# One Hymba layer on one core: key halves in all rows, tied 1/rms copies, and down's first operands in up's used tiles

## The chip, the cores and the metric

One core of a Trainium2 chip runs the kernel. Five engines take part, each with its own queue of instructions that it works off in order: TensorE (PE; its weight loads are shown apart as PEld), VectorE (DVE), ScalarE (ACT), GpSimd (POOL) and SyncE (SP), which only issues transfers. ACT and POOL issue transfers too. The metric is the device time of one execution in microseconds (us); lower is better. The instructions' times come from one profiled execution.

## What is computed

One inference step of one decoder layer, for 1024 prompt tokens and 8 x 8 decode tokens (1088 in all), width 1024, in f32. Cut to what matters:

```python
hn = rms_norm(x, norm_mix_gain)
proj = hn @ w_in                       # q,k,v,gate of retention; q,k,v of attention
o_r = rms_norm(retention(q_r, k_r, v_r, state)) * silu(g_r)
q_s = rms_norm(q_s, q_norm_gain); k_s = rms_norm(k_s, k_norm_gain)
o_s = windowed attention, 128 wide, 8 query heads on 2 key heads of 64, ALiBi, a sink logit per head
h = x + concat(o_r, o_s) @ w_out
hf = rms_norm(h, norm_ffn_gain)
h = h + square(relu(hf @ w_up)) @ w_down      # w_up 1024 x 4096, w_down 4096 x 1024
```

## The kernel before, in words

**Two halves for each f32.** PE multiplies a reduced format of f32 here (F32R). So an f32 operand is kept as a high part, rounded to that format, and a low part, the rest. `halve` (L754, L755) makes them: an ACT cast for the high one, a DVE subtraction for the low one. `mm3` (L178 to L180) is a product of two such pairs: high times high, low times high, high times low, three matmuls into one bank. Low times low is left out.

**Front.** The input is loaded and normalised. `spread` (L171 to L173) writes the tokens' 1/rms to memory (r_d) and reads them back along the free axis of all partitions (rsb). Then `proj_q` projects the first queries, and a loop over nine token tiles of 128 (L307 on) projects attention's keys and values: 24 matmuls of 256 columns into `pst`, the key's norm (hsq on ACT, hr and kn on DVE, a reciprocal root on POOL), a transposition on PE into `ptk` (L325), and the copies. `kh2[kv]` holds the high half of key head kv, 64 rows long, twice: ACT copies it (L331) to rows 0 to 63 and to rows 64 to 127. `kl` holds the low halves, one key head in each 64 rows, made by DVE (L332). All of them lie in one tile (kk).

**Attention.** `swa_block(c)` treats 128 queries, first for key head 0, then for 1, a half block each. The queries `qx` hold the high part in one half of the rows and the low part in the other (L392, L393). For each of four heads L400 multiplies all 128 rows of qx with kh2 (high and low query by high key in one matmul) and L401 the 64 high rows with the 64 rows of kl. DVE adds the bias (L402) and takes the maximum, ACT the exponentials, POOL multiplies by the reciprocal sums (L366), PE transposes the probabilities (L371) and multiplies them with the values (L420). Between these steps PE takes matmuls of other projections (psf, psg) as filler. The decode tokens come after block 7. They need `r8s`, 1/rms of the 64 decode tokens in another order, copied from rsb in 8 copies (L431); `col_sums` (L436 on) reads them.

**Up and down.** After retention and the output projection, `up(fp)` does 16 tiles of the wide MLP in a Strassen-like scheme: 7 products (PROD) on combinations of weights and activations, for two halves s of the tokens. Operands 1, 2, 6, 5, 7, 4, 3 lie in pools ops0 and ops1 as high and low tiles of 4 x 272. `left` loads a weight tile in two raw halves (`rawload`, on ACT's queue), makes the combinations on POOL (`comb`, L962) and splits them (`wsplit`). The results are squared on ACT (L1028), combined for down by four POOL subtractions for each s (L1063) and stored to u_d (L1068). Down works in five groups of 2, 4, 4, 4 and 2 such tiles; per group it does the products 1, 6, 7, 4, 5, 3, 2 (DOWN). For each it loads the activations `ur` from u_d on SP's queue (L1098), halves them into `uh` and `ul`, takes the next weight combination of each tile and issues mm3 for 4 x 2 outputs into `psd` banks; ACT copies or DVE adds them to the accumulators (L1116, L1118). In the group of two tiles a product is 4 x 2 x 2 x 3 = 48 matmuls.

**Order.** The program is written stage by stage; a scheduler with a model of the engines' times then decides, at build, the order of each engine's queue. Reading the source therefore doesn't give the order around up's end, nor of L431; the built kernel does. Tiles with the same tag share buffers: the next use waits for the last reader of the one before.

## Time and profile before

| what | before |
|---|---|
| median of 3 runs | 1283.24 us (1282.28 to 1283.95) |
| profiled execution, its span | 1280.67 us, 1278.9 us |
| mean granted PE clock | 0.981 |
| DMA | 169.45 MB, mean 133 GB/s |
| attention (100 to 300 us): PE busy | 200.00 of 200 us |

Views that are used: the page (busy time of each engine over the span); windows (busy time of each engine in a stretch, PE's granted clock as a share of full, the share of the 16 DMA engines); the timeline (start, duration, engine, line, operation, output<-inputs, and in brackets the idle time before it and what ended it); groups by line (busy time and mean ns, then idle time before them); one line's instructions (durations min/median/max in ns, rows x columns in use); waits by engine and line; and the chain, the work that led up to a point in time, step by step. A matmul's duration holds its way through the array; how fast matmuls follow one another is the difference of two starts.

### The profile page before, as it was taken

The page shows a single profiled execution, that of the slowest core. Times are in us where ns is not written, and L with a number is a line of the kernel's source. Part 1 is how long each engine was busy: PE and PEld are TensorE (multiplying, and loading weights), DVE is VectorE, ACT ScalarE, POOL GpSimd, SP SyncE. Part 2 cuts the span into 40 slices and gives each one's busy share as a digit, 9 for nine tenths or more (in the row PEclk, how much of TensorE's full clock was granted, in tenths as well). Part 3 has the DMA queues.
Part 4 walks back from the last instruction along what each step waited for, and adds up shares of the span by engine and source line. Part 5 has one row for each costly group of instructions (what it writes and reads, how often), then busy time and mean ns, then how long its engine had stood idle before and what let it go on. Part 6 is the DMA issues. An engine that isn't in the chain of part 4 may idle for free.

```text
span 1278.9 us, 23839 instructions
## 1 busy us (share of the span) xinstructions
PE 1221.7 (96%) x9621; PEld 1156.2 (90%) x9621; DVE 838.3 (66%) x1492; ACT 499.8 (39%) x1031; POOL 545.7 (43%) x463
## 2 busy tenths in 40 slices
PE   7979999999999899879999999999589999999998
PEld 5979877788979799879999999999589999999998
DVE  8735655553115787887666666766367778887766
ACT  6333343364304334444444344434264332332331
POOL 8425223123323554667565656665571321413000
PEclk9989999999989999899999999999889999999999
DMA  6211221424402944332443434333575455553124
GB/s 229 68 56 53 85 74 61 156 73 135 121 18 89 301 152 148 113 113 85 154 152 131 146 143 155 139 133 140 188 262 178 137 171 157 180 181 122 55 69 175
DMA packets 97669, 169.45 MB, mean 133 GB/s; under 512 B 11487, under 2 KB 67743, under 8 KB 97303
## 3 DMA queue, kind: packets, MB, share of 16 engines
q1 hardware_dynamic: 85783, 125.46, 29.0%
q10 hardware_dynamic: 9216, 33.56, 8.1%
q0 software_dynamic: 2560, 8.91, 2.2%
q8 instruction: 75, 1.23, 0.4%
q14 instruction: 35, 0.29, 0.1%
HBM read 114.30 MB, written 53.61 MB: 131 GB/s over the span
## 4 chain that ended last, share of the span: by engine, by line
PE 75%; DVE 9%; DMA 7%; POOL 3%; issue 3%; ACT 2%; SPq 0%; ACTq 0%; DVEq 0%; POOLq 0%
PE psd L179 8%; PE psd L180 8%; PE psd L178 8%; PE psx L178 4%; PE psx L180 4%; PE psx L179 4%; PE psf L180 3%; PE psf L178 3%; PE psf L179 3%; POOL rt L1063 2%; DMA u_d<-rt 2%; PE pst L178 2%; PE psz L178 2%; PE psz L180 2%; PE psz L179 2%
## 5 line engine op out<-in xcount | busy, mean ns | idle before, releaser
L178 PE MATMUL psd<-uh,wd_w 128*128 128x272 f32 x896 | 259.5, 290 | 17.7 <-ACT uh L754 17.7
L179 PE MATMUL psd<-uh,wd_w 128*128 128x272 f32 x896 | 260.0, 291 | 0.1
L180 PE MATMUL psd<-ul,wd_w 128*128 128x272 f32 x896 | 256.7, 289 | 0.8 <-DVE ul L755 0.8
L178 PEld LDWEIGHTS psd<-uh,wd_w 128*128 128x128 f32 x896 | 170.8, 191 | 18.1 <-ACT uh L754 18.1
L179 PEld LDWEIGHTS psd<-uh,wd_w 128*128 128x128 f32 x896 | 169.7, 189 | 0.3 <-DVE wd_w L755 0.3
L180 PEld LDWEIGHTS psd<-ul,wd_w 128*128 128x128 f32 x896 | 168.7, 189 | 1.1 <-DVE ul L755 1.1
L1118 DVE TENSOR_TENSOR a<-a,psd 128x272 f32<-128x272 f32 x248 | 102.2, 432 | 46.8 <-PE psd L180 46.7
L755 DVE TENSOR_TENSOR wu_w<-wu_s,wu_w 128x512 fp32r<-128x512 f32 x64 | 62.1, 973 | 84.6 <-ACT wu_w L754 84.4
L755 DVE TENSOR_TENSOR ul<-ur,uh 128x1088 fp32r<-128x1088 f32 x56 | 87.5, 1591 | 15.2 <-ACT uh L754 15.2
L754 ACT CAST wd_w<-wd_s 128x512 fp32r<-128x512 f32 x64 | 37.6, 621 | 112.9 <-PE psd L180 101.7
L178 PE MATMUL psx<-op_0h,wu_w 128*128 128x272 f32 x256 | 75.1, 293 | 0.7 <-ACT m L1040 0.7
L366 POOL TENSOR_TENSOR sp<-sp,ssp 128x1024 f32<-128x1024 f32 (+1 forms) x16 | 28.6, 1789 | 109.9 <-DVE ssp L365 109.9
L180 PE MATMUL psx<-op_0l,wu_w 128*128 128x272 f32 x256 | 74.3, 290 | 0.0
L178 PE MATMUL psx<-op_1h,wu_w 128*128 128x272 f32 x256 | 74.3, 290 | 0.0
L180 PE MATMUL psx<-op_1l,wu_w 128*128 128x272 f32 x256 | 74.1, 289 | 0.0
L179 PE MATMUL psx<-op_0h,wu_w 128*128 128x272 f32 x256 | 74.0, 289 | 0.0
L179 PE MATMUL psx<-op_1h,wu_w 128*128 128x272 f32 x256 | 73.7, 288 | 0.0
L754 ACT CAST uh<-ur 128x1088 fp32r<-128x1088 f32 x56 | 59.5, 1101 | 22.9 <-DMA ur<-u_d 12.4
L962 POOL TENSOR_TENSOR wd_s<-wd_r,wd_s 128x512 f32<-128x512 f32 x16 | 24.0, 1501 | 104.0 <-DVE wd_w L755 101.7
L1027 DVE SCALAR_TENSOR_TENSOR m<-m,rsf 128x272 f32<-128x272 f32 x96 | 65.5, 683 | 3.1
L180 PE MATMUL psf<-hnl,wqk_hi 128*128 128x384 f32 (+1 forms) x192 | 64.9, 338 | 0.0
L178 PE MATMUL psf<-hnh,wqk_hi 128*128 128x384 f32 (+1 forms) x192 | 64.8, 338 | 0.0
(318 smaller groups left out, 3818.8 us busy)
## 6 DMA issues: line engine op xcount, KB each, us to landing
u_d<-rt SPq DMA_DIRECT2D x32, 952.0 KB, 6.1
ur<-u_d SPq DMA_DIRECT2D x56, 544.0 KB, 5.0
wu_r<-in_w_up ACTq DMA_DIRECT2D x32, 512.0 KB, 4.3
wd_r<-in_w_down ACTq DMA_DIRECT2D x32, 512.0 KB, 5.9
y<-in_xY POOLq DMA_DIRECT2D x16, 272.0 KB, 3.3
y_d<-y POOLq DMA_DIRECT2D x16, 272.0 KB, 3.7
yt<-y_d SPq DMA_DIRECT2D x16, 272.0 KB, 3.3
out_yT<-a SPq DMA_DIRECT2D x16, 272.0 KB, 2.2
```

The costliest lines, as they stand in the source:

```text
L178: nc.tensor.matmul(ps, lh, rh, start=first, stop=False, skip_group_check=more)
L179: nc.tensor.matmul(ps, ll, rh, start=False, stop=False, skip_group_check=more)
L180: nc.tensor.matmul(ps, lh, rl, start=False, stop=last, skip_group_check=more)
L366: nc.gpsimd.tensor_tensor(s, s, ss.unsqueeze(2).broadcast_to([P, 4, n]), ALU.mult)
L754: nc.scalar.copy(hi, src)
L755: lo_eng.tensor_tensor(lo, src, hi.bitcast(F32), ALU.subtract)
L962: nc.gpsimd.tensor_tensor(t_, p_, q_, op)
L1027: nc.vector.scalar_tensor_tensor(t_, src, 0.0, rsf[:, s, h, :], ALU.max, ALU.mult)
L1063: sub = lambda o_, p_, q_: nc.gpsimd.tensor_tensor(o_, p_, q_, ALU.subtract)
L1118: nc.vector.tensor_tensor(to, to, ps, ALU.add)
```

## The change

Three edits. First, the 8 copies of L431 are tied behind the DVE instruction that ends `swa_block(5)`. Second, the low half of the keys is kept for each key head in all 128 rows (a second tile, `kl`, beside the old place), so DVE makes four subtractions for each of 8 token tiles instead of two, and the second score matmul takes all rows of qx; with this it also adds low query times low key, which was left out before. Third, the pool `ope` takes the tiles of the s = 0 operands 1, 2, 6 and 5 and outlives up. In the last `up(15)`, `first_down(1, ...)` behind product 2 and `first_down(6, ...)` behind product 5 read the activations of down's products 1 and 6 (from u_d[0], the first two tiles) and the two raw halves of the second weight tile w_down[1] into four of those tiles each, on ACT's queue, and halve the activations there. In down's groups the raw weights of all tiles but a group's first then cycle through these 8 tiles instead of 9 buffers of their own.

```diff
@@ -297,7 +297,7 @@
         square_sum(rsb[:, 768:1088], xs[2][:, k, :], k, "m2")
     sl8 = slot(8, F32R, "kk")
     kh2 = [sl8[:, kv * 1024 : kv * 1024 + 1024] for kv in range(2)]
-    kl = sl8[:, 2048:3072]
+    kl2 = [sl8[:, 2048:3072], sp.tile([P, 1024], F32R, tag="kl", name="kl", bufs=1)]
     for c, (c0, cw) in enumerate(CH):
         acc = rsb[:, c0 : c0 + cw]
         inv_rms(acc, OFFS[c], rst[:, 3 * c : 3 * c + 3], f"m{c}")
@@ -329,9 +329,9 @@
                 p_ = slice(kv * 64, kv * 64 + 64)
                 for d_ in (p_, slice(64 - kv * 64, 128 - kv * 64)):
                     nc.scalar.activation(kh2[kv][d_, cols], pt[p_], AF.Copy, scale=qkg[p_, 1:2])
-                nc.vector.scalar_tensor_tensor(
-                    kl[p_, cols], pt[p_], qkg[p_, 1:2], kh2[kv][p_, cols].bitcast(F32), ALU.mult, ALU.subtract
-                )
+                    nc.vector.scalar_tensor_tensor(
+                        kl2[kv][d_, cols], pt[p_], qkg[p_, 1:2], kh2[kv][p_, cols].bitcast(F32), ALU.mult, ALU.subtract
+                    )
             nc.vector.tensor_scalar(vs[:, t, :], ps[:, 128:256], rt, None, ALU.mult)
         if t == 7:
             nc.vector.tensor_scalar(k8[:, 0:128], pt, qkg[:, 1:2], None, ALU.mult)
@@ -398,7 +398,7 @@
                 for g in (2 * gg, 2 * gg + 1):
                     pg = ps[:, (g % 2) * 256 : (g % 2) * 256 + n]
                     nc.tensor.matmul(pg, qx[:, g, :], kh2[kv][:, k0 : k0 + n], start=True, stop=False)
-                    nc.tensor.matmul(pg, qx[p_, g, :], kl[p_, k0 : k0 + n], start=False, stop=True)
+                    nc.tensor.matmul(pg, qx[:, g, :], kl2[kv][:, k0 : k0 + n], start=False, stop=True)
                     nc.vector.scalar_tensor_tensor(
                         s[:, g, :], dtab[:, 256 - n :], nsl[:, c, kv, g : g + 1], pg, ALU.mult, ALU.add
                     )
@@ -421,17 +421,17 @@
                     po[p_, :], vs[:, c - 1 + h, p_], pts[kv][:, h, :], start=h == halves[0], stop=h == 1
                 )
         nc.scalar.copy(mh, po)
-        nc.vector.tensor_tensor(ml, po, mh.bitcast(F32), ALU.subtract)
+        ins = nc.vector.tensor_tensor(ml, po, mh.bitcast(F32), ALU.subtract)
         mix_store(mh, ml, c * 128, 128)
-
-    for c in range(NB):
-        swa_block(c)
-
-    for c_ in range(8):
-        nc.vector.tensor_copy(
-            r8s[0:1, :, :].rearrange("p t (b c i) -> p t b c i", b=2, c=8)[:, :, :, c_, :],
-            rsb[0:1, 1024:1088].rearrange("p (t b i) -> p t b i", t=4, b=2),
-        )
+        return ins
+
+    done_swa = [swa_block(c) for c in range(NB)]
+    with tc.issue_after(done_swa[5].ins):
+        for c_ in range(8):
+            nc.vector.tensor_copy(
+                r8s[0:1, :, :].rearrange("p t (b c i) -> p t b c i", b=2, c=8)[:, :, :, c_, :],
+                rsb[0:1, 1024:1088].rearrange("p (t b i) -> p t b i", t=4, b=2),
+            )
 
 
     pr = psB.tile([P, 512], F32, tag="t2", name="prq8")
@@ -760,7 +760,12 @@
         return w
 
     def rawload(src, name, tag="raw", pl=None):
-        raw = (pl or mw).tile([P, 1024], F32, tag=tag, name=name, bufs=9 if tag == "rawb" else 3)
+        if tag == "rawb":
+            t_ = ope.tile([P, 4, Q], F32, tag="op" + ("1h", "6h", "2h", "2l", "5h", "5l", "6l", "1l")[kept[0] % 8], name=name)
+            raw = t_.rearrange("p k n -> p (k n)")[:, :1024]
+            kept[0] += 1
+        else:
+            raw = mw.tile([P, 1024], F32, tag=tag, name=name, bufs=3)
         nc.scalar.dma_start(raw, src)
         return raw
 
@@ -942,18 +947,22 @@
 
     opx = ExitStack()
     ops = [[None, None] for _ in range(7)]
+    ope = ctx.enter_context(pool("ope", side="left"))
+    kept = [0]
 
     def operand_tiles(s):
         opp = opx.enter_context(pool(f"ops{s}", side="left"))
-        for i in PROD:
+        for n, i in enumerate(PROD):
             ops[RIGHT[i]][s] = [
-                opp.tile([P, 4, Q], F32R, tag=f"op{i}{x}", name=f"op{RIGHT[i]}_{s}{x}") for x in "hl"
+                (ope if s == 0 and n < 4 else opp).tile([P, 4, Q], F32R, tag=f"op{i}{x}", name=f"op{RIGHT[i]}_{s}{x}")
+                for x in "hl"
             ]
 
-    def left(order, src, name, lo_eng, raw_tag="raw", raw_pool=None, s_tag="S", s_pool=None, tags=("wa", "wb")):
-
-        r1 = rawload(src[:, :1024], f"{name}_r1", raw_tag, raw_pool)
-        r2 = rawload(src[:, 1024:], f"{name}_r2", raw_tag, raw_pool)
+    def left(order, src, name, lo_eng, raw_tag="raw", raw_pool=None, s_tag="S", s_pool=None, tags=("wa", "wb"), raws=None):
+
+        r1, r2 = raws or (
+            rawload(src[:, i * 1024 : i * 1024 + 1024], f"{name}_r{i + 1}", raw_tag, raw_pool) for i in range(2)
+        )
         a11, a12, a21, a22 = r1[:, :512], r1[:, 512:], r2[:, :512], r2[:, 512:]
         have = {1: a11, 2: a12, 4: a22}
 
@@ -1055,6 +1064,10 @@
                 if i == 4:
                     act(tq("v", s), bk, s, 0, rt[s][:, B21, :])
                     held["v", s] = None
+                if fp == 15 and s == 1 and i == 2:
+                    first_down(1, ("1h", "1l", "2h", "2l"))
+                if fp == 15 and s == 1 and i == 5:
+                    first_down(6, ("6h", "6l", "5h", "5l"))
                 if i == 3:
                     t_ = add(6, s, bk)
                     r12 = um.tile([P, Q], F32, tag="r12", name=f"r12{fp}_{s}", bufs=2)
@@ -1067,6 +1080,24 @@
                     sub(r[:, T4, :], r[:, B21, :], r[:, T2, :])
                     nc.sync.dma_start(u_d[fp // 2][:, fp % 2, s, :, :], r)
 
+    begun, raws1 = {}, []
+
+    def first_down(j, tags):
+
+
+        u_raw, raw, u_hi, u_lo = (
+            ope.tile([P, 4, Q], dt, tag="op" + tag, name=f"{n}0_{j}")
+            for n, tag, dt in zip(("ur", "rw", "uh", "ul"), tags, (F32, F32, F32R, F32R))
+        )
+        u_hi, u_lo, u_raw = (v.rearrange("p (f s) n -> p f s n", f=2) for v in (u_hi, u_lo, u_raw))
+        nc.scalar.dma_start(u_raw, u_d[0][:, :, :, RIGHT[j], :])
+        raw = raw.rearrange("p k n -> p (k n)")[:, :1024]
+        h = len(raws1) * 1024
+        nc.scalar.dma_start(raw, a["w_down"][1][:, h : h + 1024])
+        raws1.append(raw)
+        halve(u_hi, u_lo, u_raw, nc.vector)
+        begun[j] = u_hi, u_lo
+
     for fp in range(16):
         up(fp)
     opx.close()
@@ -1083,18 +1114,23 @@
         ur = dn.tile([P, 4, 2, Q], F32, tag="ur", name=f"ur{g}_{i}", bufs=2)
         return ur, [dn.tile([P, 4, 2, Q], F32R, tag=f"u{x}", name=f"u{x}{g}_{i}", bufs=2) for x in "hl"]
 
-    first_tiles = act_tiles(0, 1)
+    first_tiles = act_tiles(0, 7)
     accs[0] = dn.tile([P, 4, 2, Q], F32, tag="a0", name="a0")
     for g, (f0, nf) in enumerate(((0, 2), (2, 4), (6, 4), (10, 4), (14, 2))):
         gens = []
         for f in range(nf):
             own = ("rawb", dn, "Sb", dn) if f else ("raw", mw, "S", mid)
-            gens.append(left(DOWN, a["w_down"][f0 + f], f"wd{f0 + f}", nc.vector, *own, tags=("wb" if f % 2 else "wa",)))
+            gens.append(left(
+                DOWN, a["w_down"][f0 + f], f"wd{f0 + f}", nc.vector, *own, tags=("wb" if f % 2 else "wa",),
+                raws=raws1 if (g, f) == (0, 1) else None))
         banks = {}
         for i in DOWN:
             ws = [next(gen) for gen in gens]
-            ur, uu = first_tiles if g == 0 and i == 1 else act_tiles(g, i)
-            for f in range(0, nf, 2):
+            if g == 0 and i in begun:
+                uu = begun[i]
+            else:
+                ur, uu = first_tiles if g == 0 and i == 7 else act_tiles(g, i)
+            for f in () if g == 0 and i in begun else range(0, nf, 2):
                 nc.sync.dma_start(ur[:, f : f + 2], u_d[(f0 + f) // 2][:, :, :, RIGHT[i], :])
                 halve(uu[0][:, f : f + 2], uu[1][:, f : f + 2], ur[:, f : f + 2], nc.vector)
             q_ = INTO[i]
```

Where instructions go. DVE in the key stage, before (kn, the key times its 1/rms, is what PE transposes; hr and hsq belong to the norm of a key; q2v holds r8s and the values):

```order
L318 TENSOR_SCALAR hr<-hr,rst 128x2 [waits Pool_49]
L320 TENSOR_TENSOR kn<-pst,hr 128x128 [waits DVE_49,PE_49]
L335 TENSOR_SCALAR q2v<-pst,rst 128x128
L332 SCALAR_TENSOR_TENSOR kk<-ptk,c_qkg,kk 64x128 [waits PE_49,Activation_49]
L431 COPY q2v<-rsb 1x8x8 [waits DMAHW5_49]
L431 COPY q2v<-rsb 1x8x8 x3
L315 TENSOR_REDUCE hr<-hsq 128x2 [waits Activation_49]
L431 COPY q2v<-rsb 1x8x8 x4
```

and DVE in the changed kernel, where the copies stand now, at the end of attention's sixth block (row 359 of the queue, where before they began at row 82; ml is the low part of a block's output):

```order
L393 TENSOR_TENSOR qxp_1_2059<-q2v,qxp_1_2059 64x512 [waits Activation_49]
L351 TENSOR_REDUCE mxp_1_1974<-sp_1_1959 128x4 [waits DVE_49]
L424 TENSOR_TENSOR ml_1806<-po_1899,mh_1805 128x512 [waits DMAHW1_49,Activation_49]
L431 COPY q2v<-rsb 1x8x8 x8
L353 TENSOR_TENSOR mxp_1_1974<-mxp_1_1974,rq 128x4 [waits DVE_49]
L413 COPY ptp_0_1943<-ppp_0_1950 128x512 [waits PE_49]
```

The copies left the place between a tile's L332 and the next tile's L315, with the wait for the transfer.

ACT at up's end, before (m715_1 is a copy of up's product 7, which frees a bank for PE; rt15_0, rt15_1 and r1215_0, r1215_1 are squared results of the last tile, the latter two those that POOL's subtractions wait for; wd2_r2 and wd3_r2 are raw halves of down's third and fourth weight tiles):

```order
L1040 COPY m715_1_10098<-psx1_9927 128x272 [waits PE_49]
L754 CAST wd0_w7_10353<-wd0_s7_10351 128x512
L1028 ACTIVATE rt15_0_9932<-m715_0_10081 128x272 [waits DVE_49]
L1028 ACTIVATE rt15_1_9933<-m715_1_10098 128x272 [waits DVE_49]
L1028 ACTIVATE rt15_0_9932<-v15_0_10118 128x272 [waits DVE_49]
L1028 ACTIVATE r1215_0_10154<-m615_0_10021 128x272 [waits DVE_49,Activation_49]
L754 CAST wd0_w4_10424<-wd0_r2_10195 128x512 [waits DMAHW6_49,PE_49]
L1028 ACTIVATE rt15_1_9933<-v15_1_10133 128x272 [waits DVE_49]
L764 DMA wd2_r2_10719<-in_w_down 128x1024 [waits DVE_49]
L1028 ACTIVATE r1215_1_10175<-m615_1_10035 128x272 [waits DVE_49]
```

and in the changed kernel (uh0_6 is the high half of the activations of group 0, product 6, cast from ur0_6):

```order
L754 CAST uh0_6_10094<-ur0_6_10092 128x1088 [waits DMAHW5_49]
L1049 COPY m715_1_10134<-psx1_9947 128x272 [waits PE_49]
L754 CAST wd0_w7_10376<-wd0_s7_10374 128x512
L1037 ACTIVATE rt15_0_9952<-m715_0_10117 128x272 [waits DVE_49]
L769 DMA wd3_r2_10746<-in_w_down 128x1024 [waits DVE_49]
L1037 ACTIVATE rt15_1_9953<-m115_1_9987 128x272 [waits DMAHW6_49,Pool_49]
L1037 ACTIVATE rt15_1_9953<-m715_1_10134 128x272 [waits DVE_49]
L1037 ACTIVATE rt15_0_9952<-v15_0_10154 128x272 [waits DVE_49]
L754 CAST wd0_w4_10444<-wd0_r2_10231 128x512 [waits PE_49]
L1037 ACTIVATE rt15_1_9953<-v15_1_10169 128x272 [waits DVE_49]
L769 DMA wd2_r2_10739<-in_w_down 128x1024 [waits DVE_49]
L1037 ACTIVATE r1215_0_10190<-m615_0_10049 128x272 [waits DVE_49]
```

The cast uh0_6 now stands between the copies of up's product 7 (uh0_1 stands 9 rows ahead of it, where before the first uh came at row 769, behind all these). The load of wd3_r2 now stands ahead of r1215_0 and waits for DVE: its buffer held ur0_6, so that DVE's subtraction ul0_6 has to be done first.

POOL behind up's last tile, before (rt15_0 and rt15_1 are the two halves of the last tile's results, wd1_s6 is combination 6 of down's second weight tile, raw halves wd1_r1 and wd1_r2):

```order
L1063 TENSOR_TENSOR rt15_1_9933<-r1215_1_10175,rt15_1_9933 128x272 [waits DMAHW2_49,Activation_49]
L1063 TENSOR_TENSOR rt15_1_9933<-rt15_1_9933,r1215_1_10175 128x272
L1063 TENSOR_TENSOR rt15_1_9933<-rt15_1_9933 128x272 [waits Pool_49]
L962 TENSOR_TENSOR wd2_s5_10866<-wd2_r2_10719 128x512 [waits DMAHW3_49,DVE_49]
L1063 TENSOR_TENSOR rt15_1_9933<-rt15_1_9933 128x272 [waits Pool_49]
L962 TENSOR_TENSOR wd2_s6_10868<-wd2_s5_10866,wd2_r1_10717 128x512 [waits DMAHW0_49,DVE_49,Pool_49]
L962 TENSOR_TENSOR wd1_s5_10281<-wd1_r2_10202 128x512 [waits DMAHW0_49,PE_49]
L962 TENSOR_TENSOR wd1_s6_10283<-wd1_s5_10281,wd1_r1_10200 128x512 [waits DMAHW5_49,PE_49,Pool_49]
```

and in the changed kernel (the raw halves of that tile are now rw0_1 and rw0_6):

```order
L971 TENSOR_TENSOR wd2_s5_10886<-wd2_r2_10739 128x512 [waits DMAHW1_49,DVE_49]
L1076 TENSOR_TENSOR rt15_1_9953<-r1215_1_10211,rt15_1_9953 128x272 [waits DMAHW6_49,Activation_49]
L1076 TENSOR_TENSOR rt15_1_9953<-rt15_1_9953,r1215_1_10211 128x272
L1076 TENSOR_TENSOR rt15_0_9952<-rt15_0_9952 128x272 [waits Pool_49]
L971 TENSOR_TENSOR wd2_s6_10888<-wd2_s5_10886,wd2_r1_10737 128x512 [waits DMAHW2_49,DVE_49,Pool_49]
L1076 TENSOR_TENSOR rt15_1_9953<-rt15_1_9953 128x272 [waits Pool_49]
L971 TENSOR_TENSOR wd1_s5_10310<-rw0_6_10093 128x512 [waits DMAHW7_49,PE_49]
L971 TENSOR_TENSOR wd2_s7_11027<-wd2_r1_10737,wd2_r2_10739 128x512 [waits DVE_49]
L1076 TENSOR_TENSOR rt15_1_9953<-rt15_1_9953 128x272 [waits Pool_49]
L971 TENSOR_TENSOR wd1_s6_10312<-wd1_s5_10310,rw0_1_10023 128x512 [waits PE_49,Pool_49]
```

The eight subtractions and the combinations 5 and 6 of the third weight tile (wd2) stand ahead of wd1_s6 in both; new ahead of it is wd2_s7, and wd2_s5 moved up ahead of rt15_1.

## The prediction

> **What bounds the kernel now.** I read the page first, then windows over the stretches where the page's slices drop, then the timeline, waits and chain inside them. The page's first part:
>
> ```profile
> span 1278.9 us, 23839 instructions
> PE 1221.7 (96%) x9621; PEld 1156.2 (90%) x9621; DVE 838.3 (66%) x1492; ACT 499.8 (39%) x1031; POOL 545.7 (43%) x463
> ```
>
> PE is busy for 1221.7 of 1278.9 us, no other engine for more than 66%. Time comes off in two ways only: where PE idles (57 us in all), and where PE is busy but its matmuls follow one another slower than they could. The windows show both:
>
> ```profile
> 60.00:80.00 20.00, 13.35 (x97) 13.15 (x96) 7.98 (x36) 7.09 (x20) 2.79 (x4) 0.83 0.08 29
> ...
> 180.00:200.00 20.00, 20.00 (x102) 15.04 (x101) 9.45 (x20) 7.22 (x22) 7.09 (x4) 1.00 0.26 90
> ...
> 920.00:925.00 5.00, 0.00 (x0) 0.00 (x0) 0.00 (x0) 0.00 (x0) 1.87 (x2) 0.50 0.95 375
> ...
> 930.00:935.00 5.00, 5.00 (x22) 5.00 (x23) 3.81 (x3) 2.24 (x3) 2.38 (x3) 0.50 1.02 418
> 935.00:940.00 5.00, 5.00 (x38) 5.00 (x38) 4.03 (x4) 3.49 (x10) 2.18 (x1) 0.89 1.03 397
> ```
>
> Columns: length; PE, PEld, DVE, ACT, POOL busy; granted clock; DMA share; GB/s. In the key stage (60 to 80) PE idles 6.65 us and the clock falls to 0.83; in attention (180 to 200) PE is never idle, so that only cheaper matmuls help; at up's end everything stands still, with the DMA engines full. Each part of the change works on one of these three.
>
> **Part one, the 1/rms copies (L431).** DVE's and PE's timelines and the chain of waits around 68 us:
>
> ```profile
> 62.83 0.34 DVE L332 SCALAR_TENSOR_TENSOR kk<-ptk,c_qkg,kk 64x128 fp32r<-64x128 f32 x1
> 72.38 0.49 DVE L431 COPY q2v<-rsb 1x64 f32<-1x64 f32 x4 [9.21 <-DMA rsb<-r_d]
> ```
>
> ```profile
> 67.98 0.28 PE L179 MATMUL pst<-wkv_hi,hnl 128*128 128x256 f32 x1
> 68.10 0.28 PE L180 MATMUL pst<-wkv_lo,hnh 128*128 128x256 f32 x1
> 75.03 0.47 PE L325 MATMUL ptk<-c_ident,kn 128*128 128x128 f32 x1 [6.65 <-DVE kn L320]
> ...
> 75.52 0.41 PE L179 MATMUL pst<-wkv_hi,hnl 128*128 128x256 f32 x1
> 75.73 0.41 PE L180 MATMUL pst<-wkv_lo,hnh 128*128 128x256 f32 x1
> ...
> 79.14 0.36 PE L178 MATMUL pst<-wkv_hi,hnh 128*128 128x256 f32 x1
> ```
>
> ```profile
> 58.29 10.41 DMA r_d<-rst
> 68.79 3.56 DMA rsb<-r_d
> ```
>
> The copies sit in DVE's queue between two token tiles' key work and wait 9.21 us for the spread of 1/rms through memory (10.41 + 3.56 us). DVE is in order, so kn waits behind them and PE's transpose waits for kn: 6.65 us. Then from 75.03 to 79.14 PE runs at half clock: 0.21 us between starts where 0.12 was usual, some 19 matmuls, 1.8 us. The change puts the copies 270 rows later, behind the sixth attention block, by when the spread has long landed; their readers stand later still. **8.5 us** go. What is late next there is the key work itself, with 16 more DVE instructions (part two):
>
> ```profile
> L331 ACT ACTIVATE kk<-ptk,c_qkg 64x128 fp32r<-64x128 f32 x32 | 11.6, 363 | 18.1 <-DVE kk L332 10.5 <-PE ptk L325 7.3
> ...
> L332 DVE SCALAR_TENSOR_TENSOR kk<-ptk,c_qkg,kk 64x128 fp32r<-64x128 f32 x16 | 5.6, 348 | 5.6 <-ACT kk L331 5.5
> ```
>
> (ACT's row is of ACT's groups, DVE's of DVE's, both from 56 to 100 us.) Sixteen more at 0.348 are 5.6 us of DVE spread over the stage, 0.7 for each token tile, and DVE is busy for only 7.98 of the 20 us above. PE's 24 matmuls of a tile at 0.12 take 2.9. ACT's copies already wait for DVE's (10.5 us): should all four copies and four subtractions of a tile alternate strictly, they take 4 x (0.36 + 0.35) = 2.9 us, even with PE. So I book nothing, at worst a handover's 0.4 us for each of 8 tiles, 3 us.
>
> **Part two, the key's low half in all rows (L401).** One isolated pair of score matmuls in PE's timeline, and the line's own row:
>
> ```profile
> 200.81 0.34 PE L178 MATMUL psf<-hnh,wqk_hi 128*128 128x384 f32 x1
> ...
> 202.39 0.34 PE L178 MATMUL psf<-hnh,wqk_hi 128*128 128x384 f32 x1
> 202.57 0.28 PE L400 MATMUL scp<-kk,qxp 128*128 128x256 f32 x1
> 202.77 0.38 PE L401 MATMUL scp<-kk,qxp 64*128 64x256 f32 x1
> 203.08 0.45 PE L179 MATMUL psf<-hnh,wqk_lo 128*128 128x384 f32 x1
> 203.37 0.34 PE L180 MATMUL psf<-hnl,wqk_hi 128*128 128x384 f32 x1
> ```
>
> ```profile
> L401 PE MATMUL scp<-kk,qxp x64: 323/380/383, 103.0 to 293.1; 64*128 64x256 f32 x56, 64*128 64x128 f32 x8
> ```
>
> Full-row matmuls of 384 columns follow at 0.175 us (nine from 200.81 to 202.39), of 256 columns at 0.12 (part one). From 202.57 to 203.37 stand L400, L401 and one of 384 columns: 0.80 us, where 0.12 + 0.12 + 0.175 = 0.415 would do. The 64-row matmul is dear at both ends: 0.20 before it starts, 0.31 for itself, 0.29 for its successor. After the change all three contract 128 rows, so 0.385 goes for each pair. The fixed ends make most of it, so I take the same for the 8 of 128 columns: 64 x 0.385 = **24.6 us**. The subtractions that fill the second low tile were costed above.
>
> The Trainium skill ("TensorEngine Tiling (Array Packing)", Key Properties) says that a change of tiling mode drains TensorE, which fits the extra at both ends. Against it stands "TensorE: Matmul & The Clock Gate", Part 2, where the gap between matmuls goes by the columns streamed and not by the rows; by that alone 128 rows cost what 64 do, part two gives nothing and the sum is rival (4)'s. The traced 0.31 beside 0.12 speaks for the first, and with it for 24.6.
>
> Cover: PE must find its filler matmuls as before. The probabilities come back from POOL (L366) and are transposed by PE (L371); the tightest place I found:
>
> ```profile
> 130.82 1.04 POOL L366 TENSOR_TENSOR sp<-sp,ssp 128x512 f32<-128x512 f32 x1 [3.85 <-DVE ssp L365]
> ...
> 134.34 0.60 PE L371 MATMUL ppp<-c_ident,sp 128*128 128x128 f32 x4
> ```
>
> POOL ends at 131.86, PE reaches the transposes at 134.34: 2.5 us of slack, while a half block (four pairs) now takes 1.5 us less PE time. So most waits stay hidden, and some of the 16 may show. Ends: 0 (slack holds everywhere) and 12 us (every second half block is held by its softmax chain); I take 2, near the lower, since the slack measured is above 1.5. Net **22.6 us**.
>
> **Part three, the way from up to down.** PE at up's end, and later inside down's first group:
>
> ```profile
> 914.03 0.29 PE L179 MATMUL psz<-op_1h,wu_w 128*128 128x272 f32 x1
> 914.16 0.29 PE L180 MATMUL psz<-op_1l,wu_w 128*128 128x272 f32 x1
> ...
> 929.98 0.59 PE L178 MATMUL psd<-uh,wd_w 128*128 128x272 f32 x1 [15.54 <-ACT uh L754]
> ```
>
> ```profile
> 944.74 0.28 PE L180 MATMUL psd<-ul,wd_w 128*128 128x272 f32 x1
> 947.15 0.40 PE L178 MATMUL psd<-uh,wd_w 128*128 128x272 f32 x1 [2.13 <-ACT uh L754]
> ...
> 949.13 0.29 PE L179 MATMUL psd<-uh,wd_w 128*128 128x272 f32 x1
> 950.27 0.39 PE L180 MATMUL psd<-ul,wd_w 128*128 128x272 f32 x1 [0.85 <-DVE ul L755]
> ```
>
> Matmuls of 272 columns follow at 0.126 us. Lost now: 15.7 us from 914.29 to 929.98; 2.4 at half clock (the windows count 22 + 38 matmuls from 930 to 940, where 79 fit); 2.3 before 947.15 and 1.0 before 950.27. Together **21.4 us**. The wait is ACT's uh for the activations, which are stored, read back and queued among weight loads with the DMA engines full:
>
> ```profile
> ACT uh L754 <- DMA ur<-u_d: 12.4, 1, 12.4
> ```
>
> The change reads u_d[0] (stored long before) during up's last tile. By the new order of PE, 12 matmuls of down's product 1 run before up's last two products and 36 behind them; with up's end shifted 1.5 us (12 x 0.126) product 1 ends near 914.3 + 6.0 = 920.3. Product 6 needs two weight combinations. That of tile 0 is ready. PE waits about 1.5 us for ACT (a cast of 0.6 us, then the accumulator copies of 0.4 that free the banks), and does 24 matmuls with it, to 925. That of tile 1, wd1_s6, stands late in POOL's queue: behind eight subtractions of up's last tile, two combinations of tile 2, wd1_s5 and wd2_s7. Their prices:
>
> ```profile
> L1063 POOL TENSOR_TENSOR rt<-rt 128x272 f32<-128x272 f32 x4 | 3.1, 774 | 0.1
> ...
> L962 POOL TENSOR_TENSOR wd_s<-wd_s,wd_r 128x512 f32<-128x512 f32 x1 | 1.3, 1253 | 0.0
> ```
>
> ```profile
> 916.54 0.75 POOL L1063 TENSOR_TENSOR rt<-r,rt 128x272 f32<-128x272 f32 x1
> ```
>
> That row was before's second half (the first began at 912.98 by the same view). Now the first begins there too: r1215_0, which it waits for, stands in ACT's queue behind the load of wd3_r2, and that waits until DVE has subtracted ul0_6, whose cast starts behind up's last copies. 8 x 0.78 + 5 x 1.25 = 12.5 us: wd1_s6 is there at 929, after a wait for tile 2's load perhaps at 930.5; cast (0.6) to 931. PE stands from 925 to 931, **6 us**, and the clock halves again, for some 2 us more (19 matmuls cost 1.8 in part one). Lost after the change: 1.5 + 6 + 2 = 9.5, so **11.9 us** are gained. Ends: 20 if POOL's work comes in time, -1 if tile 2's load and the casts in ACT's in-order queue hold up everything as long as now.
>
> **The sum.** 8.5 + 22.6 + 11.9 = 43.0 us. The profiled execution took 1280.67 us (span 1278.9 and 1.8 around it): 1237.7. The median of the runs, 1283.24, is 2.6 above it, which I add: **1240.3 us**.
>
> **The rivals.** (1) The softmax chain becomes the bound: POOL's multiplication waits for DVE at every half block, so PE may run out of filler. For it: the slack of 2.5; against: PE 20.00 of 20 and DVE 9.45. Half of part two's 24.6 is lost instead of 2: 1250.6. (2) No new stall in product 6, POOL being earlier than I walk it: the 8 us of wait and half clock stay away: 1232. (3) The transition stays as long, because ACT takes uh in order ahead of copies that free up's banks, and POOL starts later: 1252, with nothing of the 11.9. (4) L401's 0.31 comes from something other than its 64 rows, such as accumulating onto L400's bank: part two gives nothing, 1240.3 + 22.6 = 1263. For it: the second of two in one bank waits; against: L179 and L180 accumulate in the same way at 0.12. (5) Slower than before: the key stage locks. ACT's copies and DVE's subtractions go to one shared tile, and ACT already waits for DVE there; if each of 8 instructions of a tile waits for the one before with a handover, and hsq and kn of the next tile stand behind them in both queues, a tile's turn becomes their sum. It costs more than it brings from 43.0/8 = 5.4 us for each of 8 tiles beyond PE's 2.9, that is from a turn of 8.3 us; at 10 us a turn the time is 1240.3 + 8 x 7.1 = 1297. The durations of 0.36 and 0.35 speak against: eight of them make 2.9. (6) The change has no effect: the copies still wait, or the loads wait for the operands' last use until up ends: 1283; the new order shows them ahead.
>
> **Chances.** Forecast 0.60; (1) 0.13; (2) 0.10; (3) 0.10; (4) 0.03; (5) 0.03; (6) 0.01. The forecast's own spread is about 4 us either way, from the key stage (3), the score chain and a slightly changed order in retention. For 8 in 10 the range takes in (1), (2) and (3): 1230 to 1253. Faster by over 0.2% (2.6 us, about what a measurement of this kernel tells from no change) 0.96, within 0.01, slower 0.03.
>
> **What would show it.** Right: no wait for L431 and full clock from 60 to 80; the low score matmul listed with 128 rows and about 0.12 us to its successor; psd matmuls among up's psx and psz; one PE wait of about 6 us for wd1_w6's cast, with half clock behind it. Wrong: PE below 20 of 20 in windows of attention, waits of PE for ACT kk, or a wait for uh as long as now.

## The result, and the profile after

| | before | changed |
|---|---|---|
| median (range) of 4 runs, us | 1282.76 (1281.4 to 1283.95) | 1244.31 (1242.84 to 1246.85) |
| profiled execution, its span, us | 1280.67, 1278.9 | 1243.79, 1242.0 |

The ratio is 0.9703, with a 95% interval from 0.9683 to 0.9722: 38.1 us faster (35.7 to 40.7). 1240.3 was forecast, and the time lies in the range. A second set of runs of the changed kernel gave 0.9723 (0.9707 to 0.9739).

The page of the changed kernel, its first part:

```profile
span 1242.0 us, 23874 instructions
## 1 busy us (share of the span) xinstructions
PE 1195.2 (96%) x9621; PEld 1148.6 (92%) x9621; DVE 845.7 (68%) x1508; ACT 505.7 (41%) x1035; POOL 550.8 (44%) x463
```

PE has the same 9621 matmuls and is busy 26.5 us less: these matmuls follow one another faster. The other 10.4 us of the span are idle time that went. The windows (columns as in the prediction) of the key stage, of attention and of the transition:

```profile
60.00:80.00 20.00, 20.00 (x155) 19.96 (x155) 14.66 (x50) 12.30 (x32) 7.17 (x7) 1.00 0.12 37
...
180.00:200.00 20.00, 20.00 (x123) 18.05 (x121) 15.23 (x24) 9.97 (x25) 6.62 (x3) 1.00 0.24 81
```

```profile
900.00:905.00 5.00, 0.00 (x0) 0.00 (x0) 4.46 (x3) 1.01 (x2) 5.00 (x3) 0.86 0.60 227
905.00:910.00 5.00, 3.72 (x16) 3.72 (x17) 3.60 (x3) 2.66 (x5) 5.00 (x4) 0.50 1.02 327
```

From 60 to 80 us PE is never idle and at full clock. From 180 to 200 it gets 123 matmuls done where it did 102. From 900 to 905 it stands still, and half clock follows: the wait that the prediction put into product 6.

Where the 36.9 us of the profiled executions lie, I read from the starts of the same matmul in two timelines (the last transposition of a key, the 301st of up's psx, the first of down's second group, the last one of all), in us against before:

```
                          before   alone: 1st  2nd    3rd   1st+2nd  changed  again
last key transposition     94.02      -8.5   +1.6   +0.5     -8.3     -8.6    -8.5
up, matmul 301 of psx     639.21      -8.7  -20.3   +3.9    -25.2    -27.8   -25.3
first of down's group 2   978.55      -8.5  -21.4   -3.8    -25.9    -37.1   -31.9
last matmul              1274.74      -8.6  -21.8   -4.1    -26.3    -36.9   -31.8
```

Key stage 8.6, from there to up's steady state 19.1, transition 9.3. The last two columns are one kernel, executed twice: the places of the gains agree, but their sizes differ by 2.5 us ahead of up and 2.7 us at the transition. The 2.5 us fit the clock: from the last key transposition to up's 301st matmul PE idles 24.2 us in one profile and 23.6 in the other, but half clock was granted for 23.9 us of it in one and for 34.1 in the other. Differences of that size between single profiles say nothing of the edits.

### The profile page after: what moved, and what is told of

Read it like the earlier page. It is cut to its first block, busy times and chain, and to the rows that moved or that the text cites. A ratio compares the mean times of both kernels' runs of the same rounds, so it can differ in the third digit from the quotient of the medians.

```text
span 1242.0 us, 23874 instructions
## 1 busy us (share of the span) xinstructions
PE 1195.2 (96%) x9621; PEld 1148.6 (92%) x9621; DVE 845.7 (68%) x1508; ACT 505.7 (41%) x1035; POOL 550.8 (44%) x463
## 4 chain that ended last, share of the span: by engine, by line
PE 62%; DVE 7%; DMA 4%; issue 2%; ACT 2%; POOL 2%; SPq 0%; DVEq 0%; POOLq 0%; ACTq 0%
PE psd L179 8%; PE psd L178 8%; PE psd L180 8%; PE psx L179 5%; PE psx L180 5%; PE psx L178 5%; PE psz L180 2%; PE psz L179 2%; PE psz L178 2%; DMA wor_raw<-in_w_out 2%; PE pst L178 1%; PE pst L179 1%; PE pst L180 1%; DVE op_0l L755 1%; PE psy L178 1%
## 5 line engine op out<-in xcount | busy, mean ns | idle before, releaser
L755 DVE TENSOR_TENSOR ul<-ur,uh 128x1088 fp32r<-128x1088 f32 x56 | 83.9, 1526 | 4.2 <-ACT uh L754 4.2
L1076 POOL TENSOR_TENSOR rt<-rt 128x272 f32<-128x272 f32 x64 | 65.6, 1036 | 1.1
L755 DVE TENSOR_TENSOR wd_w<-wd_s,wd_w 128x512 fp32r<-128x512 f32 x64 | 54.6, 867 | 15.6 <-ACT wd_w L754 15.5
```

The lines of the kernel that those rows point to most:

```text
L755: lo_eng.tensor_tensor(lo, src, hi.bitcast(F32), ALU.subtract)
L1076: sub = lambda o_, p_, q_: nc.gpsimd.tensor_tensor(o_, p_, q_, ALU.subtract)
```

## The experiments

**The three parts alone.** The kernel before, with one part of the diff each. For the first part:

> The kernel before with the tied 1/rms copies alone. Theory: the wait of 9.2 us in VectorE's queue and the half clock behind it go, as the changed kernel shows between its first projections and the end of the key stage (8.7 us earlier): ratio to before 0.9932, 1274 us. Rival: the key work is slow enough to give half of it back later (softmax chain or output projection as the next limit): 0.9966, 1278.4 us.

Measured: 1271.69 us, ratio 0.9914 (0.9893 to 0.9935), and 8.6 us in the profiled execution, all of it gained by the end of the key stage and none given back. The theory holds; by the medians the gain is 11.0 us, with an interval from 8.3 to 13.7. For the second:

> The kernel before with the key's low halves in all rows alone. The scores' matmuls and their successors take 24.4 us less in the changed kernel's trace, but from the end of the key stage to up's steady state it gained only 19.0. Theory 1: the 5.4 us are lost by waits that come with shorter attention blocks, so they are lost here too: 1264 us, ratio 0.985. Theory 2: they are lost through the tied copies or by chance in the scheduler's order: 1258.5 us, 0.981. Rival: extra subtractions hold up the key stage: PE waits there by 3 us or more, 1267 us.

Measured: 1258.07 us, ratio 0.9801 (0.9784 to 0.9817): 25.5 us, theory 2. Its profile has 21.8: 21.9 from the key stage to up's steady state, and 1.6 lost in the key stage, where the 1/rms copies are still in VectorE's way and PE waits 7.3 us instead of 6.7. For the third:

> The kernel before with the transition alone. Theory: gains 9.3 us as the changed kernel did between up's steady state and down's second group, with the same waits of about 2 us (copy of product 7 behind the cast of the activations on ScalarE) and 8 us (combination 6 of the second weight tile, late on GpSimd): 1273.4 us, 0.9927. Rival: the waits come from the state in which the other two parts leave the queues, and alone it gains 15 us or more: 1267 us.

Measured: 1273.37 us, ratio 0.9919 (0.9901 to 0.9937): 10.4 us, as forecast; its profile, of the run with the highest time of the four, has 4.1, with waits of 3.4 and 5.9 us where 2 and 8 were expected. The three gains add to 46.9 us where the changed kernel has 38.1. So first and second together were run (the diff's first two parts):

> Parts one and two together, without the transition. The three parts alone gave 11.0, 25.5 and 10.4 us, 46.9 in all, the changed kernel 38.1. Theory 1: one and two add up (36.5 us, ratio 0.9715, 1247 us), and the transition is worth only some 3 us in company, because its tiles change the order and the waits ahead of up (3.9 us later at up's steady state in its own trace) as well as the end. Theory 2: one and two don't add up (both shorten the way to the same attention waits): 28 to 30 us, 1253 us, and the transition keeps its 9 to 10.

Measured: 1254.46 us, ratio 0.9775 (0.9758 to 0.9791), 28.9 us of 36.5: theory 2 has the size. Parts one and two don't add up, and 7.6 us are missing (some 4 us either way, by the three intervals; 4.1 in the profiled executions: 8.6 + 21.8 against 26.3). Three waits of PE that neither part has alone in this size show up. The timeline of the two parts together at up's first operands, and PE's waits by engine and line from 60 to 345 us:

```profile
532.67 0.40 PE L179 MATMUL psx<-op_0h,wu_w 128*128 128x272 f32 x1 [2.95 <-DVE wu_w L755]
```

```profile
PE pst L178 <- ACT vtr L578: 1.9, 1, 1.9
PE po L420 <- ACT ptp L411: 1.1, 1, 1.1
```

The second part alone has 0.3 and 0.5 us for the latter two and 0.5 for wu_w. VectorE's wait for the residual input ahead of up's first operands is not what is new; in the changed kernel and in the kernel before:

```profile
523.51 0.79 DVE L802 TENSOR_TENSOR y<-pso,y 128x272 f32<-128x272 f32 x2 [2.98 <-DMA y<-in_xY]
```

```profile
553.14 0.79 DVE L797 TENSOR_TENSOR y<-pso,y 128x272 f32<-128x272 f32 x2 [2.50 <-DMA y<-in_xY]
```

Summed over all of PE's rows from the last key transposition to up's 301st matmul, PE idles 18.9 us before, 18.8 with the first part alone, 20.3 with the second and 23.2 with both. That is 2.9 us more than the parts would add up to, of 5.1 that are lost in this stretch (1.4 come back in the key stage, where the second part alone loses its 1.6). The rest fits the half clock, granted for 34.1 us of the stretch with both parts and for 23.9 and 27.3 with one. Neither share was shown by taking it away, and the waits aren't all bound to the two parts: the one for vtr is 1.9 us too with the scores at 64 rows (next run), and four of the later variants of the changed kernel don't have the one for wu_w.

**Rows or something else.** In the changed kernel only the second score matmul goes back to 64 rows:

```diff
-                    nc.tensor.matmul(pg, qx[:, g, :], kl2[kv][:, k0 : k0 + n], start=False, stop=True)
+                    nc.tensor.matmul(pg, qx[p_, g, :], kl2[kv][p_, k0 : k0 + n], start=False, stop=True)
```

> The changed kernel with the second score matmul put back to 64 rows; the low halves are still made for all rows. (It leaves out low query times low key, as before.) Theory: the 64 rows themselves cost 0.385 us for each of 64 pairs, so all of part two goes, and the extra subtractions cost nothing: 1244.3 + 19 to 24 = 1263 to 1269 us. Rival: what cost 0.31 us was not the rows: 1244 us, and the gain in attention came from something else.

Measured: 1267.46 us, ratio 0.9876 (0.9859 to 0.9892): by the ratios 22.2 us above the changed kernel, and 19.6 above its second set of runs. The 64 rows among full ones were the price. Its key stage ends within 0.3 us of that of the first part alone, though VectorE makes the 16 additional subtractions, so these cost PE nothing. The changed kernel's scores at full rows, in PE's timeline:

```profile
232.07 0.28 PE L400 MATMUL scp<-kk,qxp 128*128 128x256 f32 x1
232.18 0.29 PE L401 MATMUL scp<-kk,qxp 128*128 128x256 f32 x1
232.30 0.28 PE L400 MATMUL scp<-kk,qxp 128*128 128x256 f32 x1
232.42 0.28 PE L401 MATMUL scp<-kk,qxp 128*128 128x256 f32 x1
232.54 0.34 PE L180 MATMUL psg<-hnl,wg_hi 128*128 128x384 f32 x1
```

Four matmuls in 0.47 us, 0.12 each. Added up over all 64 pairs and their successors, from start to next start, 48.9 us became 24.6. In the run with 64 rows they take 47.8.

**What holds up the transition.** Six variants of the changed kernel follow. PE's idle times there, from its timeline:

```profile
884.55 0.39 PE L178 MATMUL psx<-op_1h,wu_w 128*128 128x272 f32 x1 [2.02 <-ACT m L1049]
...
895.10 0.39 PE L178 MATMUL psd<-uh,wd_w 128*128 128x272 f32 x1 [1.21 <-ACT a L1152]
...
906.28 2.18 PE L178 MATMUL psd<-uh,wd_w 128*128 128x272 f32 x8 [7.92 <-ACT wd_w L754]
```

The 7.92 is the wait for combination 6 of down's second weight tile. First, its four combinations on VectorE (a tile with preloaded raw halves has `raws`):

```diff
-            nc.gpsimd.tensor_tensor(t_, p_, q_, op)
+            (nc.vector if raws else nc.gpsimd).tensor_tensor(t_, p_, q_, op)
```

> The changed kernel, with the four combinations of down's second weight tile made by VectorE instead of GpSimd. Theory: TensorE's wait of 7.9 us in product 6 is GpSimd's queue (the last tile's subtractions and the third tile's combinations ahead of wd1_s6). On VectorE the combination is there before the first half of product 6 ends, the wait falls below 1 us, the half clock behind it (1.9 us) goes, and up to 2 us come back as a wait for the low activations of product 7, which stand behind the combinations on VectorE: 1236 us, ratio to the changed kernel 0.993. Rival: the transfers are the limit (the raw half or the activations land late), the wait stays: 1244 us.

Measured: 1249.6 us, ratio 0.9742 (0.9729 to 0.9756), slower than the changed kernel (0.9703), though not clear of the noise against its second set of runs (0.9723). The wait fell to 0.7 us as expected, but others came, in PE's waits from 875 to 960 us and VectorE's timeline:

```profile
PE psd L178 <- ACT a L1152: 6.0, 3, 4.2
PE psd L180 <- DVE ul L755: 2.2, 1, 2.2
PE psd L179 <- DVE wd_w L755: 2.1, 1, 2.1
```

```profile
894.35 1.27 DVE L971 TENSOR_TENSOR wd_s<-rw 128x512 f32<-128x512 f32 x1
895.65 1.15 DVE L971 TENSOR_TENSOR wd_s<-wd_s,rw 128x512 f32<-128x512 f32 x1
896.73 1.24 DVE L971 TENSOR_TENSOR wd_s<-rw,rw 128x512 f32<-128x512 f32 x1
897.89 1.77 DVE L971 TENSOR_TENSOR wd_s<-rw,wd_s 128x512 f32<-128x512 f32 x1
...
902.45 1.76 DVE L755 TENSOR_TENSOR wd_w<-rw,wd_w 128x512 fp32r<-128x512 f32 x1
```

In the changed kernel VectorE's timeline has the same operation on a weight while GpSimd rests:

```profile
885.80 0.69 DVE L755 TENSOR_TENSOR wd_w<-wd_s,wd_w 128x512 fp32r<-128x512 f32 x1
```

0.69 us there, 1.76 us beside a busy GpSimd. VectorE was free but not fast. My expectation had only counted instructions. The waits alone don't make the loss, though: from up's 301st matmul to down's second group they sum to 12.3 us against 11.2 in the changed kernel. Half clock lasted longer, and over matmuls instead of a wait. With the four combinations on VectorE, windows:

```profile
905.00:910.00 5.00, 2.78 (x10) 2.46 (x11) 5.00 (x4) 3.24 (x9) 5.00 (x3) 0.50 0.81 232
910.00:915.00 5.00, 5.00 (x23) 5.00 (x23) 3.31 (x2) 0.00 (x0) 3.29 (x3) 0.50 1.03 405
```

PE is busy at half clock for 14.4 us in that stretch, in the changed kernel for 4.2. Second, the cast of product 6's activations tied on ScalarE behind the copies of up's product 7 (`copied` is the latter; up to there the cast and its subtraction are put off):

```diff
-                    nc.scalar.copy(t_, bk)
+                    copied = nc.scalar.copy(t_, bk)
...
+                if fp == 15 and s == 1 and i == 7:
+                    with tc.issue_after(copied.ins):
+                        late6()
```

> The changed kernel, with the cast of product 6's activations tied behind ScalarE's copies of up's product 7. Theory: the wait of 2.0 us before up's product 4 (TensorE for the copy, which stands behind a cast that waits 4.0 us for its transfer) goes, and everything behind it, GpSimd's subtractions too, moves ahead by as much: 1242.3 us. Rival: the wait turns up again at product 6, whose combination depends on GpSimd's queue and on the transfers: 1244 us.

Measured: 1243.17 us, ratio 0.9692 (0.9679 to 0.9705), not to be told from the changed kernel. The 2.0 us wait is gone and product 6 waits 10.1 us instead of 7.9: the rival, the wait only moves. Third, both edits:

> The changed kernel with both mends. Theory: the two waits are one behind the other on TensorE's way, so their gains add: 1234 us, ratio to the changed kernel 0.992. Rival: with TensorE earlier by 2 us, VectorE's combinations or the activations of product 7 are late by as much: 1236 us.

Measured: 1246.97 us, ratio 0.9724 (0.9703 to 0.9746). Neither theory: the waits are those of the first edit (ScalarE's accumulator copies 6.5 us, VectorE's low halves 5.1 us). Fourth, the combinations 5 and 6 made earlier, by GpSimd, in the 15 us in which it idles, with the changed kernel run again for comparison:

```diff
+        if j == 6:
+            t_ = ope.tile([P, 4, Q], F32, tag="op1h", name="wd1_s56").rearrange("p k n -> p (k n)")
+            kept[0] += 1
+            made[5], made[6] = t_[:, :512], t_[:, 512:1024]
+            nc.gpsimd.tensor_tensor(made[5], raw[:, :512], raw[:, 512:], ALU.add)
+            nc.gpsimd.tensor_tensor(made[6], made[5], raws1[0][:, :512], ALU.subtract)
```

> The changed kernel again, as the measure for the next two, on their chip. Expected: 1243 to 1246 us, ratio to before 0.970.

Measured: 1246.31 us, ratio 0.9723 (0.9707 to 0.9739).

> The changed kernel, with combinations 5 and 6 of down's second weight tile written into a used operand tile by GpSimd while it idles during up's last products (15.4 us idle before 890.25 us in the changed kernel's trace), ahead of the last tile's subtractions. Theory: the price of the move to VectorE was VectorE itself, whose operations took 1.2 to 1.8 us instead of 0.7 beside a busy GpSimd; here neither engine gets more work in that stretch, so the wait of 7.9 us and its half clock (1.9 us) go and at most 3 us come back at product 7: ratio to the changed kernel 0.993 to 0.995, 1236 to 1239 us. Rival: what stands behind it, the low activations and the casts of products 7 and 4, needs as long whatever the weights do, so that the wait only moves, as with VectorE: 1244 us or more.

Measured: 1245.91 us, ratio 0.9714 (0.9694 to 0.9735): the rival. PE doesn't wait in product 6 at all, but 8.0 us at product 4. PE's waits from 875 to 960 us, and the chain up to that place:

```profile
PE psd L178 <- ACT a L1158: 8.7, 2, 8.0
PE psx L178 <- ACT m L1049: 2.2, 1, 2.2
```

```profile
901.77 5.76 POOL wd_s L971 x3
907.54 1.19 POOL rt L1076
908.72 0.02 issue
908.74 8.69 DMA u_d<-rt
```

ScalarE can't copy product 7 to its accumulator, because that takes the buffer of the last tile's results (tag g1 in the code), and these are not stored: their last subtraction stands on GpSimd behind combinations of weights, three of them in this piece of the chain. With the cast behind product 7's copies as well:

> The same with the cast of product 6's activations behind ScalarE's copies of up's product 7. Theory: with the combination early, the 2.0 us saved at up's product 7 are no longer taken back at product 6: 2 us below the kernel with the early combinations alone. Rival: they are taken back at product 7: the same.

Measured: 1249.17 us, ratio 0.9737 (0.9719 to 0.9756), no gain; PE now waits 4.1 us for uh, 2.1 for ul and 5.4 for the accumulator copies. So the last edit put the eight subtractions first, on top of the early combinations:

```diff
-                    sub(r[:, T4, :], r[:, B21, :], r[:, T2, :])
+                    last_sub[0] = sub(r[:, T4, :], r[:, B21, :], r[:, T2, :])
...
-            nc.gpsimd.tensor_tensor(t_, p_, q_, op)
+            with tc.issue_after(last_sub[0].ins) if name in ("wd1", "wd2", "wd3") else ExitStack():
+                nc.gpsimd.tensor_tensor(t_, p_, q_, op)
```

> The early combinations, and on GpSimd the last tile's eight subtractions ahead of all other combinations. With the early combinations alone TensorE's wait stood at the start of product 4 (8.2 us): the accumulator of product 7 takes the buffer of the last tile's results, whose store (8.7 us) began when the last subtraction ended, at 908.7 us, behind five combinations. Theory: with the subtractions first the store begins 8 us earlier and the wait falls to some 2 us (two weight casts still stand ahead of the copies on ScalarE); 4 to 6 us below the kernel with the early combinations, 1240 to 1242 us, ratio to before 0.967 to 0.968. Rival: what stands behind it again (the low activations of product 5 on VectorE, slowed by GpSimd) takes most of it back: 1244 us, ratio 0.970.

Measured: 1237.84 us (1236.69 to 1239.52), ratio 0.9652 (0.9639 to 0.9665). It lies below both kernels and below the forecast of 1240 to 1242. By the ratios it beats the changed kernel by 6.5 us, and by 9.1 against its second set of runs. GpSimd's and PE's sides of it (timeline, PE's waits from 870 to 960 us):

```profile
892.91 0.75 POOL L1077 TENSOR_TENSOR rt<-rt,r 128x272 f32<-128x272 f32 x1
893.62 2.79 POOL L1077 TENSOR_TENSOR rt<-rt 128x272 f32<-128x272 f32 x3
896.38 1.29 POOL L972 TENSOR_TENSOR wd_s<-rw,rw 128x512 f32<-128x512 f32 x1
```

```profile
PE psd L178 <- ACT uh L754: 2.2, 1, 2.2
PE psd L178 <- ACT a L1159: 1.8, 2, 1.1
PE psx L178 <- ACT m L1050: 1.3, 1, 1.3
```

The last subtraction ends at 896.4 instead of 908.7, and PE's waits at the transition sum to 5.3 us instead of 11.2. So two orders on GpSimd held the transition: the one that the prediction named, and one that shows when the first is mended. The subtractions first without the early combinations were not run, so that it isn't shown whether this edit alone would have done.

The transition in all these runs, from up's 301st matmul to the first of down's second group, summed over PE's rows and the granted clock in each trace (us):

| | time | PE idle | PE busy at half clock |
|---|---|---|---|
| before | 339.3 | 19.1 | 6.1 |
| changed | 330.0 | 11.2 | 4.2 |
| changed, again | 332.7 | 12.8 | 5.7 |
| second tile's combinations on VectorE | 336.6 | 12.3 | 14.4 |
| cast behind product 7's copies | 330.0 | 11.3 | 4.4 |
| both of these | 333.9 | 12.3 | 6.8 |
| early combinations | 331.1 | 11.9 | 4.1 |
| early combinations, cast behind | 337.4 | 13.4 | 13.2 |
| early combinations, subtractions first | 324.6 | 5.2 | 3.4 |

At half clock matmuls of 272 columns follow at 0.23 us instead of 0.126 (by their starts behind 906.28 us in the changed kernel). The time less the idle time and half of the busy time at half clock is 316.5 to 318.2 us in every row. So these two make nearly all the differences: the edits that failed moved the idle time without making it shorter, and the two slowest of the variants lost most by the clock.

## Why the prediction was right, point by point

- **The 1/rms copies, 8.5 us.** 8.6 us in the trace, with full clock from 60 to 80. Right, also that the 16 additional subtractions are covered, at least once the copies are out of their way.
- **The low score matmul, 24.6 us.** 24.3 us by starts; 20 to 22 when only this is undone. Rival (4), something other than the rows, is out.
- **The 2 us of friction in attention.** The mechanism was other: the transpositions' slack held, and rival (1), the softmax chain as the bound, shows in a 1.1 us wait only. PE's idle time grew by 1.7 us in attention, so that PE is at 198.33 of 200 us from 100 to 300 us, which was named as a sign of being wrong, and by 3.6 us between attention and up. The term was too small by 3.3 us, and most of the loss lies outside the stage that it was booked in.
- **The transition, 11.9 us.** 9.3 and 6.6 us in two profiled executions. Right in kind: the copies' wait (1.5 forecast, 1.2 measured), then combination 6 and half clock behind it (16 and 17 matmuls and weight loads from 905 to 910). Mis-sized were the wait, 7.9 and 9.5 us where 6 was summed, and a wait of 2.0 us that the sum didn't have: a cast waits 4.0 us for its transfer at the head of ScalarE's queue. I had named that queue only as a rival. GpSimd took 15.3 us from its first subtraction (890.25) to the end of combination 6 (905.58) where 12.5 was summed, and the 1.5 us that were added for a late load didn't come. One combination took 2.3 us where 1.25 was used; VectorE was busy beside it:

```profile
903.28 2.30 POOL L971 TENSOR_TENSOR wd_s<-wd_s,rw 128x512 f32<-128x512 f32 x1
```

- **Slower than before, rival (5).** Nothing of it showed: PE is busy 20.00 of 20 us in the key stage.

The changed kernel took 4.0 us more than forecast. Between the profiled executions 43.0 us were forecast and 36.9 came, 6.1 less: 3.5 ahead of up, 2.6 in the transition. Of these 6.1, 2.1 don't show in the median, by chance: the sum adds 2.6 us because before's profiled run was that much faster than its median, and the changed kernel's was only 0.5 faster. So the close hit of the time is in part luck.

What stays open: the transition alone came with 3.9 us more ahead of up in its one profile, 3.0 of them idle time of PE, and in company two profiles of one kernel differ there by 2.5 us. Whether its tiles make the waits at up's first operands longer can't be told from this.

## What to carry to other kernels

When one engine is busy all the time, read the distance between the starts of its instructions, not their durations: the mixed row counts cost 0.385 us a pair and stood in no wait. Gains of separate edits add only as far as the other engines' order leaves room; here 36.5 us of two edits gave 28.9. And behind a wait that is taken away look for the next in the same queue before giving the work to another engine: moving four instructions from GpSimd to VectorE lost some 2 to 5 us, ordering GpSimd's instructions by who needs them first gained 6.5 to 9. Last, sum the idle time and the time at half clock apart: a wait that is cut into pieces can cost more by the clock than it did whole.

## What the runs showed of the hardware

- VectorE and GpSimd slow each other. Over the fourteen traces the low half of one of down's weights (128x512, f32) took 0.67 to 0.69 us on VectorE in all 1103 cases without any GpSimd work beside it, and 0.68 to 1.81, half of them over 1.4, where GpSimd's combinations ran beside it nearly all the time. A combination took 1.25 to 1.32 us alone and up to 2.4 beside such subtractions, half of them over 1.7. The Trainium skill ("GPSIMD Engine Reference", 1. Specifications) says that GpSimd's interfaces to SBUF are shared with VectorE, with contention where VectorE's instruction has two SBUF inputs, as these have. The runs agree, and the price of up to 2.6 times is theirs. They show the other side too: VectorE's additions to the accumulators, which read one of their inputs from a psd bank, took 0.42 to 0.44 us with or without GpSimd beside them, and combinations beside these alone 1.28 to 1.30.
- A matmul on 64 of 128 rows among full ones took 0.31 us instead of 0.12 to its successor's start, delayed its own start by 0.08 us and its successor's successor by 0.11 us. With full rows all three extras were gone.
- One kernel's executions differ in where PE's clock halves: from the last key transposition to down's second group the changed kernel's two profiles have 35.3 and 36.3 us of idle time of PE, but PE is busy at half clock for 23.0 us in one and 33.1 in the other. They lie 5.1 us apart there.
